# A two-layer hybrid trunk: a block end that transposes x times a scale known one sub-layer ahead

## The chip, the cores and the metric

One core of a Trainium2 chip runs the whole program. The metric is the device time of one execution in microseconds; the figure of a kernel is the median of its runs.

## What is computed

A trunk of two layers over 512 tokens of 1024 features, all in fp32: layer 0 mixes tokens by differential attention, layer 1 by a short gated convolution, and each mixer is followed by a squared-ReLU MLP with 4096 hidden features. Every sub-layer is wrapped in two RMS norms, one ahead of it and one behind it. Shapes left out, it is:

```python
def rmsnorm(x, g):
    return x * lax.rsqrt(jnp.mean(x * x, axis=-1, keepdims=True) + EPS) * g

def short_conv(x, w_in, conv_w, w_out):
    b_gate, c_gate, v = jnp.split(x @ w_in, 3, axis=-1)
    u = c_gate * v                      
    y = conv_w[0] * shift(u, 2) + conv_w[1] * shift(u, 1) + conv_w[2] * u
    return (b_gate * y) @ w_out

def reference(x, ...):
    for i in range(2):
        h = rmsnorm(x, norm_mixer_pre[i])
        m = diff_attention(h, ...) if i == 0 else short_conv(h, ...)
        x = x + rmsnorm(m, norm_mixer_post[i])
        h = rmsnorm(x, norm_mlp_pre[i])
        x = x + rmsnorm(jnp.square(jax.nn.relu(h @ w_up[i])) @ w_down[i], norm_mlp_post[i])
    return x
```

Two facts of it matter here. A norm's factor is one number for each token. And the sub-layers are homogeneous in their input: the MLP and the conv's product `b_gate * c_gate * v` scale with a power of a token's factor (the MLP with the square), and the norm behind the sub-layer divides such a factor out again, but for EPS.

## The kernel before

Every fp32 product is made of three matmuls of rounded parts, hi x hi, lo x hi and hi x lo (`mm3`, lines 66 to 70). ScalarE casts the hi half, VectorE subtracts it from the source for the lo half (`split`, line 199; lines 201 and 202). The stages follow each other in one program: the projections for v and for q and k of eight heads, attention in 32 units, `wo` (the output projection of attention), the MLP of layer 0 (m0), `ci` (the conv's input projection, 24 tiles), `wc` (its output projection) and the MLP of layer 1 (m1). The MLPs' down projection works in seven groups of products into pairs of PSUM banks x, y and z (`down`), which VectorE adds into `acc` (`into`, line 735), and a tail (`tail`) of four token blocks.

`wo`, m0, `wc` and m1 end in `block_end` (line 602), once for each of four blocks of 128 tokens, which applies the norm behind the sub-layer, adds to the residual `x_sb`, applies the norm ahead of the next sub-layer, and has TensorE turn the result into hT, the next stage's operand. Before the change its chain is: two products with `g_post` (line 618), two squares on ScalarE (line 610), two adds on VectorE (lines 612 and 74), a pow on POOL (line 75), x in two halves (line 623); then the same again for x, two squares, two adds and a pow, and hn in two halves (line 632). `turn` holds eight transposes (line 640), two casts on ScalarE for hT_hi (line 643) and two subtractions on VectorE for hT_lo (line 644). It is put into the program some 14 to 22 matmul triples later, by `after`; a scheduler then orders each engine's instructions, and each engine works through its own list in that order.

The first norm (of x itself) is different: v, q and k are projected from x times g, and the token's factor r0 is multiplied in later. For q and k that is in the rope tables, which lie with tokens along the free axis. So r0 has to stand as a row in all partitions, which is a product of a matrix of ones with a diagonal:

```python
    for b in range(NB):
        POOL.tensor_scalar(dg[:, b * P:(b + 1) * P], ident, r0[:, b:b + 1], None, op0=ALU.mult)
    ...
        for b in range(NB):
            PE.matmul(r_ps[:, b * P:(b + 1) * P], lhsT=ones, rhs=dg[:, b * P:(b + 1) * P], start=True, stop=True)
        for j in range(2):
            DVE.tensor_tensor(ropes[:, j], r_ps, ropes[:, j], op=ALU.mult)
```

All loads and stores are issued by SP's queue, in the order of the program.

Of the kernel before, what the change touches and what calls it, by code (L numbers as in the profile page):

```python
# [17 lines left out]
P = 128  # L18
# [24 lines left out]
def trunk(ctx: ExitStack, tc: tile.TileContext, x, xT, w_qk, w_v, w_o, w_in, w_out,  # L43
# [7 lines left out]
    st = ctx.enter_context(tc.tile_pool(name="st", bufs=4))  # L51
    ps = ctx.enter_context(tc.tile_pool(name="ps", bufs=1, space=bass.MemoryType.PSUM))
# [112 lines left out]
    def issue():  # L165
        while n_issued[0] < len(loads):
# [21 lines left out]
            for p in range(2 if first else 1):  # L188
# [5 lines left out]
                if n == "v" and i == p == 0:  # L194
                    nc.sync.dma_start(col, cols)
# [91 lines left out]

    issue()
# [160 lines left out]
    def wo_end(b, o):  # L449
        block_end(f"wo{b}", b, o, norm_rows[0], norm_rows[1], (16, 16, 20, 22)[b])  # L450
# [141 lines left out]
    allowed.append("rawd")  # L592
    issue()
# [8 lines left out]
    def block_end(name, b, parts, g_post, g_next, wait, last=False, cuts=(slice(0, 512), slice(512, 1024))):  # L602


        def mean_square(srcs, tag):

            ss = [small(f"{tag}_{name}_{n}") for n in range(len(srcs))]
            for n, src in enumerate(srcs):
                junk = late.tile([P, 8, 256], F32, tag="F", name=f"jk{tag}_{name}_{n}", bufs=1)
                ACT.activation(junk.rearrange("p a b -> p (a b)")[:, :src.shape[-1]], src, AF.Square, scale=D ** -0.5, accum_out=ss[n])  # L610
                if n < len(srcs) - 1:
                    DVE.tensor_scalar(ss[n], ss[n], EPS if n == 0 else ss[n - 1], None, op0=ALU.add)  # L612
# [284 lines left out]
```

## Time and profile before

| | |
|---|---|
| median of 3 runs | 1118.2 us (1117.86 to 1119.34) |
| the profiled execution | 1119.26 us, its span 1117.4 us |
| TensorE busy | 1096.5 us, 98% |
| VectorE busy | 795.1 us, 71% |
| ScalarE busy | 530.4 us, 47% |
| POOL busy | 101.8 us, 9% |
| TensorE's clock | 0.997 of full speed in the mean |

In rows of the profile PE is TensorE's matmuls, PEld its weight loads, DVE VectorE, ACT ScalarE, POOL GpSimd and SP the queue of the loads. Times count from the start of the span. PEclk is the clock that TensorE was granted, 1.00 being 2.4 GHz and 0.50 1.2 GHz. A row of the timeline gives the start, the time from the first instruction's start to the last one's end, and in brackets how long the engine stood idle before it and what ended that.

### The profile page before, as it was taken

What the parts mean: (1) busy time and instruction counts of PE and PEld (TensorE: products, weight loads), DVE (VectorE), ACT (ScalarE), POOL (GpSimd) and SP (SyncE); (2) the same over time, 40 slices, a digit from 0 to 9 for tenths busy, and PEclk for the clock granted to TensorE, in tenths of its full rate; (3) what the DMA queues carried; (4) which work ended last, traced back from release to release, by engine and by line L of the source; (5) the groups of instructions that cost most, each with busy time, mean ns of one, the idle gap of its engine ahead of it and who ended that gap; (6) DMA issues with size and microseconds to landing.
All of it is one profiled execution on the core that took longest, in us unless ns stands there. A gap on an engine that the chain in (4) does not pass through costs nothing.

```text
span 1117.4 us, 14523 instructions
## 1 busy us (share of the span) xinstructions
PE 1096.5 (98%) x5468; PEld 920.5 (82%) x5468; DVE 795.1 (71%) x1144; ACT 530.4 (47%) x909; POOL 101.8 (9%) x147
## 2 busy tenths in 40 slices
PE   9999999999999999999998999999999999999997
PEld 7878777779888888888888988888988888888886
DVE  6598887455979778878687544446587797797766
ACT  6445555444754554554544422325375445445532
POOL 1144444211000000000001000000000000000000
PEclk9999999999999999999999999999999999999999
DMA  8654444145124314314043332214142242143202
GB/s 307 226 160 124 125 109 128 37 144 197 55 96 151 122 40 140 132 57 151 17 135 114 119 104 98 94 38 143 66 151 75 76 151 95 57 151 111 78 20 76
DMA packets 39447, 124.83 MB, mean 112 GB/s; under 512 B 5072, under 2 KB 5712, under 8 KB 39376
## 3 DMA queue, kind: packets, MB, share of 16 engines
q1 hardware_dynamic: 39376, 123.90, 33.7%
q8 instruction: 43, 0.70, 0.3%
q14 instruction: 28, 0.23, 0.1%
HBM read 111.30 MB, written 2.10 MB: 101 GB/s over the span
## 4 chain that ended last, share of the span: by engine, by line
PE 72%; DVE 3%; issue 2%; POOL 1%; ACT 1%; DMA 0%; POOLq 0%; DVEq 0%; ACTq 0%
PE bank L70 24%; PE bank L69 24%; PE bank L68 24%; DVE x_sb L623 1%; PE bank L640 1%; DVE mg_m L618 0%; DVE acc L779 0%; DVE hn_m L632 0%; DVE lo_up L202 0%; DMA raw_ci<-in_w_in 0%; DVE hT_lo L644 0%; POOL rb_wo L75 0%; POOL rb_m L75 0%; DVE hn_wo L632 0%; POOL ra_m L75 0%
## 5 line engine op out<-in xcount | busy, mean ns | idle before, releaser
L68 PE MATMUL bank<-hT_hi,hi_up 128*128 128x512 f32 (+1 forms) x608 | 216.7, 356 | 0.0
L70 PE MATMUL bank<-hT_hi,lo_up 128*128 128x512 f32 (+1 forms) x608 | 216.5, 356 | 0.0
L69 PE MATMUL bank<-hT_lo,hi_up 128*128 128x512 f32 (+1 forms) x608 | 216.4, 356 | 0.0
L69 PEld LDWEIGHTS bank<-hT_lo,hi_up 128*128 128x128 f32 x608 | 115.0, 189 | 16.3
L68 PEld LDWEIGHTS bank<-hT_hi,hi_up 128*128 128x128 f32 x608 | 115.0, 189 | 16.2
L70 PEld LDWEIGHTS bank<-hT_hi,lo_up 128*128 128x128 f32 x608 | 115.0, 189 | 16.2
L735 DVE TENSOR_TENSOR acc<-acc,bank 128x512 f32<-128x512 f32 x180 | 116.8, 683 | 4.4 <-PE bank L70 4.4
L201 ACT CAST hi_up<-raw_up 128x1024 fp32r<-128x1024 f32 x64 | 67.2, 1054 | 87.2 <-PE bank L70 76.3
L202 DVE TENSOR_TENSOR lo_up<-raw_up,hi_up 128x1024 fp32r<-128x1024 f32 x64 | 76.8, 1220 | 8.7 <-ACT hi_up L201 8.7
L202 DVE TENSOR_TENSOR lo_G<-rawd,hi_G 128x1024 fp32r<-128x1024 f32 x28 | 34.2, 1222 | 44.2 <-ACT hi_G L201 44.2
L69 PE MATMUL bank<-hT_lo,hi_ci 128*128 128x512 f32 (+1 forms) x176 | 62.6, 356 | 1.8 <-DVE b_m L612 1.8
L68 PE MATMUL bank<-hT_hi,hi_ci 128*128 128x512 f32 (+1 forms) x176 | 62.7, 356 | 0.9 <-ACT hT_hi L643 0.8
L70 PE MATMUL bank<-hT_hi,lo_ci 128*128 128x512 f32 (+1 forms) x176 | 62.4, 355 | 0.0
L685 ACT ACTIVATE F<-bank 128x512 f32<-128x512 f32 x64 | 37.6, 593 | 45.0 <-PE bank L70 35.9
L201 ACT CAST hi_G<-rawd 128x1024 fp32r<-128x1024 f32 x28 | 29.5, 1054 | 46.2 <-PE bank L69 31.1
L202 DVE TENSOR_TENSOR lo_E<-rawd,hi_E 128x1024 fp32r<-128x1024 f32 x28 | 34.2, 1222 | 23.4 <-ACT hi_E L201 23.4
L202 DVE TENSOR_TENSOR lo_A<-rawd,hi_A 128x1024 fp32r<-128x1024 f32 x28 | 33.5, 1220 | 19.5 <-ACT hi_A L201 19.5
L201 ACT CAST hi_E<-rawd 128x1024 fp32r<-128x1024 f32 x28 | 29.3, 1048 | 34.9 <-PE bank L69 33.4
L68 PE MATMUL bank<-hi_A,ua_hi 128*128 128x512 f32 x112 | 44.1, 394 | 0.0
L201 ACT CAST hi_A<-rawd 128x1024 fp32r<-128x1024 f32 x28 | 29.5, 1053 | 30.3 <-PE bank L69 17.7
L69 PE MATMUL bank<-lo_A,ua_hi 128*128 128x512 f32 x112 | 43.7, 390 | 0.0
L68 PE MATMUL bank<-hi_E,ub_hi 128*128 128x512 f32 x112 | 43.6, 390 | 0.0
(308 smaller groups left out, 2629.2 us busy)
## 6 DMA issues: line engine op xcount, KB each, us to landing
raw_up<-in_w_up SPq DMA_DIRECT2D x64, 512.0 KB, 4.0
rawd<-in_w_down SPq DMA_DIRECT2D x56, 512.0 KB, 4.4
raw_ci<-in_w_in SPq DMA_DIRECT2D x24, 512.0 KB, 3.5
raw_q<-in_w_qk SPq DMA_DIRECT2D x8, 512.0 KB, 4.5
raw_k<-in_w_qk SPq DMA_DIRECT2D x8, 512.0 KB, 4.3
q<-sw_q SPq DMA_DIRECT2D x32, 128.0 KB, 2.3
raw_wo<-in_w_o SPq DMA_DIRECT2D x8, 512.0 KB, 3.7
raw_dn<-in_w_down SPq DMA_DIRECT2D x8, 512.0 KB, 3.5
```

Of the source, the lines that this page charges most:

```text
L68: PE.matmul(o, lhsT=a[0], rhs=b[0], start=start, stop=False, skip_group_check=more)
L69: PE.matmul(o, lhsT=a[0], rhs=b[1], start=False, stop=False, skip_group_check=more)
L70: PE.matmul(o, lhsT=a[1], rhs=b[0], start=False, stop=stop, skip_group_check=more)
L201: (DVE.tensor_copy if on_dve else ACT.copy)(hi, src)
L202: DVE.tensor_tensor(lo, src, hi.bitcast(F32), op=ALU.subtract)
L623: DVE.scalar_tensor_tensor(xn, m, r, xn, op0=ALU.mult, op1=ALU.add)
L640: PE.transpose(tp[:, j * P:(j + 1) * P], hns[n][:, j * P:(j + 1) * P], ident)
L685: ACT.activation(dst, o, AF.Relu)
L735: DVE.tensor_tensor(a, a, o[t], op=op)
```

## The change

**Block ends.** hn is now x times `s` times `g_next`, where `s` is (ms + 1)^-0.5 with the mean square ms that x had one sub-layer earlier, so it is there before x is. x's own mean square is still taken, by one square of 1024 columns, but off this chain. `settle` forms from it, once a sub-layer's four blocks are done, the factor q = (ms + EPS) s^2 by which hn's square is off, and folds it into the EPS of the next norm behind a sub-layer (power 2 for the MLPs, power 1 for the conv), and for the conv also into a row 1/q, which multiplies the c gate as it leaves PSUM (VectorE, in place of ScalarE's copy). The sums of squares and EPS are added on POOL, ahead of the pow, no longer on VectorE. x and hn are done in one instruction of 1024 columns each (in m1, whose x goes out, in the cuts as before); m0's ends take one square and one product of 1024.

**Rows through memory.** The r0 row and the 1/q row are made by `along_rows`: POOL's DMA queue writes the 128x4 numbers into DRAM in the order of the tokens and reads them back into all partitions. The four `dg` products on TensorE are gone, and VectorE multiplies the rope tables from SBUF.

**Down projection.** The y pair stays in PSUM through all seven groups and into the tail, which goes on adding to it, so two of the adds into `acc` go in each group. The tail's banks are fixed by hand.

**Small ones.** `col` is loaded first, from ScalarE's queue; `rawd` loads are let in a little later.

```diff
-    def rsqrt(r, ms, eps):
-        DVE.tensor_scalar(r, ms, eps, None, op0=ALU.add)
-        POOL.tensor_tensor(r, r, mhalf[:, :ms.shape[-1]], op=ALU.pow)
-        return r
...
-                if n == "v" and i == p == 0:
-                    nc.sync.dma_start(col, cols)
...
+    nc.scalar.dma_start(col, cols)
     issue()
...
+    def along_rows(c, r, name):
+        d = dram.tile([1, T], F32, name=f"row_{name}")
+        POOL.dma_start(d.rearrange("o (b p) -> p (o b)", p=P), c)
+        POOL.dma_start(r, d.partition_broadcast(P))
+        return r
...
+    def scales(ms, name):
+        s = tokens(f"s_{name}")
+        POOL.tensor_scalar(s, ms, 1.0, None, op0=ALU.add)
+        POOL.tensor_tensor(s, s, mhalf, op=ALU.pow)
+        return s
+
+    def settle(name, nxt, power):
+        ms, s, q, e = about["ms", name], about["s", name], tokens(f"q_{name}"), tokens(f"e_{name}")
+        POOL.tensor_scalar(q, ms, EPS, None, op0=ALU.add)
+        for _ in range(2):
+            POOL.tensor_tensor(q, q, s, op=ALU.mult)
+        POOL.tensor_scalar(e, q, EPS, None, op0=ALU.mult)
+        if power == 1:
+            POOL.tensor_tensor(q, q, mone, op=ALU.pow)
+            about["row"] = along_rows(q, acc[:, 2, 0:T], "q")
+        else:
+            POOL.tensor_tensor(e, e, q, op=ALU.mult)
+        about["eps", nxt] = e
+        if nxt != "m1":
+            about["s", nxt] = scales(ms, nxt)
...
+        if kt == 6:
+            r0 = small("r0", 4)
+            POOL.tensor_scalar(r0, ss0, EPS, None, op0=ALU.add)
+            POOL.tensor_tensor(r0, r0, mhalf, op=ALU.pow)
+            about["s", "wo"] = scales(ss0, "wo")
+            r_row = along_rows(r0, t512(ap, "r_row", "c", 2), "r0")
...
-            DVE.tensor_tensor(ropes[:, j], r_ps, ropes[:, j], op=ALU.mult)
+            DVE.tensor_tensor(ropes[:, j], r_row, ropes[:, j], op=ALU.mult)
...
+        m = late.tile([P, D], F32, tag="mg", name=f"mg_{name}_{b}", bufs=1)
+        for p, c in zip(parts, cuts):
+            DVE.tensor_tensor(m[:, c], p, g_post[:, c], op=ALU.mult)
+        for n, src in enumerate(parts):
+            ss = small(f"ss_{name}_{b}_{n}")
+            mean_square(ss, src, n)
+            if n:
+                POOL.tensor_tensor(r, ss, r, op=ALU.add)
+            elif ("eps", name) in about:
+                POOL.tensor_tensor(r, ss, about["eps", name][:, b:b + 1], op=ALU.add)
+            else:
+                POOL.tensor_scalar(r, ss, EPS, None, op0=ALU.add)
+        POOL.tensor_tensor(r, r, mhalf[:, 0:1], op=ALU.pow)
+        xb = x_sb[:, b, :]
+        for c in cuts if last else (slice(0, D),):
+            DVE.scalar_tensor_tensor(xb[:, c], m[:, c], r, xb[:, c], op0=ALU.mult, op1=ALU.add)
...
-        r2 = mean_square([x_sb[:, b, c] for c in cuts], "b")
...
+        hn = late.tile([P, D], F32, tag="hn", name=f"hn_{name}_{b}", bufs=2)
+        DVE.scalar_tensor_tensor(hn, xb, about["s", name][:, b:b + 1], g_next, op0=ALU.mult, op1=ALU.mult)
+        if b == 0:
+            about["ms", name] = tokens(f"ms_{name}")
+        mean_square(about["ms", name][:, b:b + 1], xb, "x")
+        if b == NB - 1:
+            settle(name, nxt, power)
...
-            product(g, y, True, "A12", "A", 1)
-            into((1, 1), y, ALU.add)
+            product(g, y, new, "A12", "A", 1)
...
+                spare = [(z[0], z[1]), (x[0], x[1]), (y[0], z[0]), (y[1], z[1], x[0])][b]
+                spare = list(spare)
                 for run in runs:
-                    os = [bank() for c in run]
+                    os = [spare.pop(0) for c in run]
...
-            ACT.copy(held["c"], o)
+            DVE.tensor_tensor(held["c"], o, about["row"], op=ALU.mult)
```

What this does to the order of instructions is seen at three places. The first is VectorE in the projections, between the last step for lambda (`neg_lam`) and the rope tables; `lo_` and `both_` are lo halves of weights, `acc<-bank` and `acc<-pair` the evictions of v. Before:

```order
L368 TENSOR_SCALAR neg_lam<-neg_lam 128x1
L202 TENSOR_TENSOR lo_q_595<-raw_q_463,hi_q_594 128x512 x2
L202 TENSOR_TENSOR lo_k_684<-raw_k_508,hi_k_683 128x512 x2
L202 TENSOR_TENSOR both_q_780<-raw_q_555,both_q_780 128x512 x2
L348 TENSOR_SCALAR acc<-bank_71,r_424 128x512
L348 TENSOR_SCALAR acc<-pair_77,r_424 128x512
L348 TENSOR_SCALAR acc<-pair_78,r_424 128x512
L348 TENSOR_SCALAR acc<-bank_73,r_424 128x512
L202 TENSOR_TENSOR both_k_888<-raw_k_600,both_k_888 128x512 x2
L355 TENSOR_TENSOR ropes<-bank_73,ropes 128x512 x2
```

With the change:

```order
L400 TENSOR_SCALAR neg_lam<-neg_lam 128x1
L387 TENSOR_TENSOR ropes<-r_row,ropes 128x512 x2
L195 TENSOR_TENSOR lo_q_597<-raw_q_469,hi_q_596 128x512 x2
L195 TENSOR_TENSOR lo_k_686<-raw_k_510,hi_k_685 128x512 x2
L195 TENSOR_TENSOR both_q_782<-raw_q_557,both_q_782 128x512 x2
L383 TENSOR_SCALAR acc<-bank_73,r_395 128x512
```

The two rope products have moved from behind the evictions and a further pair of lo halves to ahead of three pairs and the evictions.

The second is TensorE in the last run of `wo`'s block 2, where block 0's transposes (`ident,hn_wo`) are put in. Before:

```order
L70 MATMUL pair_77<-both_wo_2079,oT_lo 128x512
L68 MATMUL pair_77<-both_wo_2079,oT_hi 128x512
L69 MATMUL pair_77<-both_wo_2079,oT_hi 128x512
L70 MATMUL pair_77<-both_wo_2079,oT_lo 128x512
L68 MATMUL pair_77<-both_wo_2105,oT_hi 128x512
L640 MATMUL bank_72<-ident,hn_wo_0_2391 128x128 x4
L69 MATMUL pair_77<-both_wo_2105,oT_hi 128x512
L640 MATMUL bank_73<-ident,hn_wo_1_2393 128x128 x4
L70 MATMUL pair_77<-both_wo_2105,oT_lo 128x512
L68 MATMUL pair_77<-both_wo_2105,oT_hi 128x512
L69 MATMUL pair_77<-both_wo_2105,oT_hi 128x512
L70 MATMUL pair_77<-both_wo_2105,oT_lo 128x512
```

With the change:

```order
L69 MATMUL pair_79<-both_wo_2081,oT_hi 128x512
L70 MATMUL pair_79<-both_wo_2081,oT_hi 128x512
L673 MATMUL bank_74<-ident,hn_wo_2381 128x128 x4
L673 MATMUL bank_75<-ident,hn_wo_2381 128x128 x4
L71 MATMUL pair_79<-both_wo_2081,oT_lo 128x512
L69 MATMUL pair_79<-both_wo_2081,oT_hi 128x512
L70 MATMUL pair_79<-both_wo_2081,oT_hi 128x512
L71 MATMUL pair_79<-both_wo_2081,oT_lo 128x512
L69 MATMUL pair_79<-both_wo_2107,oT_hi 128x512
L70 MATMUL pair_79<-both_wo_2107,oT_hi 128x512
```

The eight transposes stand together, after two matmuls of the last run of twelve instead of after seven. Those of block 1 stand 21 matmuls behind block 0's, those of block 2 33 matmuls behind block 1's.

The third is VectorE in m0's ends, from block 2's product with `g_post` to block 1's hT_lo (two instructions), the first of which TensorE needs for the conv's first tile. Before:

```order
L618 TENSOR_TENSOR mg_m_2_1_5153<-acc,g_post_2619 128x512
L612 TENSOR_SCALAR a_m_2_0_5155<-a_m_2_0_5155 128x1
L202 TENSOR_TENSOR lo_ci_5252<-raw_ci_4994,hi_ci_5251 128x1024
L74 TENSOR_SCALAR ra_m_2_5162<-a_m_2_1_5156,a_m_2_0_5155 128x1
L779 TENSOR_TENSOR acc<-bank_2617,acc 128x512
L623 SCALAR_TENSOR_TENSOR x_sb<-mg_m_2_0_5151,ra_m_2_5162,x_sb 128x512
L623 SCALAR_TENSOR_TENSOR x_sb<-mg_m_2_1_5153,ra_m_2_5162,x_sb 128x512
L644 TENSOR_TENSOR hT_lo<-bank_72,hT_hi 128x4x128
L612 TENSOR_SCALAR b_m_2_0_5167<-b_m_2_0_5167 128x1
L644 TENSOR_TENSOR hT_lo<-bank_73,hT_hi 128x4x128
```

With the change:

```order
L643 TENSOR_TENSOR mg_m_2_5070<-acc,g_post_2584 128x1024
L195 TENSOR_TENSOR lo_ci_5149<-raw_ci_4945,hi_ci_5148 128x1024
L656 SCALAR_TENSOR_TENSOR x_sb<-mg_m_2_5070,r_m_2_5069,x_sb 128x1024
L195 TENSOR_TENSOR lo_ci_5179<-raw_ci_4956,hi_ci_5178 128x1024
L662 SCALAR_TENSOR_TENSOR hn_m_2_5078<-x_sb,s_m_2573,g_pre_2586 128x1024
L677 TENSOR_TENSOR hT_lo<-bank_74,hT_hi 128x4x128
L677 TENSOR_TENSOR hT_lo<-bank_75,hT_hi 128x4x128
```

Block 1's hT_lo stood behind one `lo_ci`, an add from a bank and x in two halves; now it stands behind two `lo_ci`, x and hn, and the add comes later.

## Rows read from the trace of the kernel before

**Rows 1.** The page's first part: busy us, share of the span, instructions.

```profile
PE 1096.5 (98%) x5468; PEld 920.5 (82%) x5468; DVE 795.1 (71%) x1144; ACT 530.4 (47%) x909; POOL 101.8 (9%) x147
```

**Rows 2.** Stretches: length, busy us of each engine (instructions), PEclk, DMA share, GB/s.

```profile
220.00:240.00 20.00, 18.50 (x92) 15.15 (x91) 7.26 (x17) 5.09 (x16) 2.60 (x6) 1.00 0.44 158
230.00:237.00 7.00, 7.00 (x32) 5.81 (x31) 3.22 (x7) 2.50 (x7) 0.55 (x1) 1.00 0.99 379
...
620.00:1100.00 480.00, 480.00 (x2319) 405.20 (x2318) 323.57 (x421) 211.08 (x290) 4.94 (x9) 1.00 0.28 96
```

**Rows 3.** TensorE's waits in the whole run: who waited for whom: us, times, longest.

```profile
PE bank L640 <- DVE hn_wo L632: 2.8, 3, 1.5
PE bank L69 <- DVE b_m L612: 1.8, 1, 1.8
```

**Rows 4.** Stretches again, where m0's end meets the conv.

```profile
591.00:595.00 4.00, 1.31 (x7) 0.80 (x6) 3.87 (x8) 2.60 (x7) 0.55 (x1) 1.00 0.37 130
595.00:600.00 5.00, 5.00 (x30) 5.00 (x31) 4.87 (x9) 2.56 (x7) 0.55 (x1) 0.66 0.01 3
607.00:609.00 2.00, 1.57 (x15) 1.37 (x14) 1.42 (x2) 0.15 (x1) 0.31 (x1) 1.00 0.89 274
```

**Rows 5.** Timeline of block 0's `wo` end, VectorE and TensorE: start us, us, instruction [idle before].

```profile
235.00 1.42 DVE L623 SCALAR_TENSOR_TENSOR x_sb<-mg_wo,ra_wo,x_sb 128x512 f32<-128x512 f32 x2 [0.66 <-POOL ra_wo L75]
...
238.23 1.42 DVE L632 SCALAR_TENSOR_TENSOR hn_wo<-x_sb,rb_wo,g_pre 128x512 f32<-128x512 f32 x2
...
239.13 0.63 PE L640 MATMUL bank<-ident,hn_wo 128*128 128x128 f32 x4 [1.50 <-DVE hn_wo L632]
```

**Rows 6.** Timeline of TensorE at the `dg` products.

```profile
51.93 1.05 PE L353 MATMUL bank<-dg,ones 128*128 128x128 f32 x8
52.74 0.47 PE L68 MATMUL bank<-hT_hi,hi_q 128*128 128x512 f32 x1
```

**Rows 7.** Timeline of ScalarE: the last 1024-wide square.

```profile
32.37 1.06 ACT L332 ACTIVATE xb<-xb 128x1024 f32<-128x1024 f32 x1 [0.90 <-DMA xb<-in_x]
```

**Rows 8.** Groups by line and shape, POOL: busy us, mean ns, idle before.

```profile
L532 POOL TENSOR_SCALAR f<-eps 128x4 f32<-128x4 f32 x7 | 1.6, 228 | 0.6
```

**Rows 9.** Timeline of POOL: two of the pows.

```profile
234.42 0.55 POOL L75 TENSOR_TENSOR ra_wo<-ra_wo,mhalf 128x1 f32<-128x1 f32 x1 [8.85 <-DVE ra_wo L74]
...
247.02 1.46 POOL L75 TENSOR_TENSOR rb_wo<-rb_wo,mhalf 128x1 f32<-128x1 f32 x1 [4.04 <-DVE rb_wo L74]
```

**Rows 10.** DMA issues: count, KB each, us to landing.

```profile
x_sb<-in_x SPq DMA_DIRECT2D x4, 512.0 KB, 7.4
...
col<-in_cols SPq DMA_DIRECT2D x1, 16.5 KB, 2.7
```

**Rows 11.** Timeline of VectorE in the projections.

```profile
44.63 1.30 DVE L202 TENSOR_TENSOR both_q<-raw_q,both_q 128x512 fp32r<-128x512 f32 x2 [2.56 <-ACT both_q L201]
45.84 0.74 DVE L348 TENSOR_SCALAR acc<-bank,r 128x512 f32<-128x512 f32 x1
...
55.77 0.74 DVE L380 STREAM_SHUFFLE sw_q<-bank 128x512 f32<-128x512 f32 x1
```

**Rows 12.** Groups by line and shape, VectorE.

```profile
L735 DVE TENSOR_TENSOR acc<-acc,bank 128x512 f32<-128x512 f32 x180 | 116.8, 683 | 4.4 <-PE bank L70 4.4
L202 DVE TENSOR_TENSOR lo_up<-raw_up,hi_up 128x1024 fp32r<-128x1024 f32 x64 | 76.8, 1220 | 8.7 <-ACT hi_up L201 8.7
```

**Rows 13.** Timeline of VectorE in m0's ends.

```profile
583.94 1.41 DVE L623 SCALAR_TENSOR_TENSOR x_sb<-mg_m,ra_m,x_sb 128x512 f32<-128x512 f32 x2 [0.73 <-POOL ra_m L75]
...
594.18 0.68 DVE L644 TENSOR_TENSOR hT_lo<-bank,hT_hi 128x512 fp32r<-128x512 f32 x1
```

**Rows 14.** Timeline in the conv: ScalarE's first gate copy, TensorE's first 512-wide tile.

```profile
619.48 0.58 ACT L809 COPY conv<-bank 128x512 f32<-128x512 f32 x1
...
632.84 0.40 PE L68 MATMUL bank<-hT_hi,hi_ci 128*128 128x512 f32 x1
```

**Rows 15.** Timeline of VectorE: the last x.

```profile
1114.17 0.49 DVE L623 SCALAR_TENSOR_TENSOR x_sb<-mg_m,ra_m,x_sb 128x256 f32<-128x256 f32 x1
```

More of the change, by code (lines that the diff above doesn't have):

```diff
@@ L599, in row, with block_end, mean_square @@
         return r
[L602 to L612, printed above, removed]
-            return rsqrt(small(f"r{tag}_{name}"), ss[-1], ss[-2])
-        mg = []
-        for n, (p, c) in enumerate(zip(parts, cuts)):
-            m = t512(late, f"mg_{name}_{n}", "mg", 2)[:, :c.stop - c.start]
-            DVE.tensor_tensor(m, p, g_post[:, c], op=ALU.mult)
-            mg.append(m)
-        r = mean_square(parts, "a")
-        for m, c in zip(mg, cuts):
-            xn = x_sb[:, b, c]
-            DVE.scalar_tensor_tensor(xn, m, r, xn, op0=ALU.mult, op1=ALU.add)
+    def block_end(name, nxt, power, b, parts, g_post, g_next, wait, last=False, cuts=(slice(0, 512), slice(512, 1024))):
+        def mean_square(ss, src, n=0):
+            junk = late.tile([P, 8, 256], F32, tag="F", name=f"jk_{name}_{b}_{n}", bufs=1)
+            ACT.activation(junk.rearrange("p a b -> p (a b)")[:, :src.shape[-1]], src, AF.Square, scale=D ** -0.5, accum_out=ss)
+        r = small(f"r_{name}_{b}")
+        m = late.tile([P, D], F32, tag="mg", name=f"mg_{name}_{b}", bufs=1)
[14 more added lines that the diff above has]
+            DVE.scalar_tensor_tensor(xb[:, c], m[:, c], r, xb[:, c], op0=ALU.mult, op1=ALU.add)
@@ L716, in finish @@
                 us[n, p] = [x[:, j, :] for x in t]
+        x, y, z = ([banks[2 * i], banks[2 * i + 1]] for i in range(3))
         def product(g, o, first, form, kind, half):
@@ L725, in product @@
                     step(lambda: mm3(o[t], part(us[form, p], ALL, slice(t * P, (t + 1) * P)), part(w, ALL, s),
-                                     first and p == groups[g][0], p == groups[g][-1], not first))
+                                     first and p == groups[g][0], p == groups[g][-1] and o is not y,
+                                     not first and o is not y))
         def into(c, o, op, fresh=False):
@@ L737, in down @@
         def down(g):
-            x, y, z = ([banks[2 * i], banks[2 * i + 1]] for i in range(3))
             new, pq = g == 0, groups[g]
@@ L779, in tail @@
                         DVE.tensor_tensor(a, o, a, op=ALU.add)
-                cuts = [c for run in runs for c in run]
-                block_end(f"m{l}_{b}", b, [acc[:, b, c] for c in cuts], g_post, g_next, 14, last=l == 1, cuts=cuts)
+                cuts = [c for run in runs for c in run] if l else [slice(0, D)]
+                block_end(f"m{l}", "wc", 1, b, [acc[:, b, c] for c in cuts], g_post, g_next, 14, last=l == 1, cuts=cuts)
         for n, what in mlp_steps:
```

33 lines of the change are left out of this document (13 added, 20 removed).

## The prediction

> **What bounds the kernel now.** Read the busy times first: TensorE works in 1096.5 of 1117.4 us [rows 1]. The program is therefore as long as TensorE's own list of matmuls plus about 21 us of gaps, and an edit pays only if it takes matmuls out, closes a gap, or shortens the end behind the last matmul. The table of stretches then says where gaps can be: from 620 to 1100 us TensorE is busy in all 480.00 us, though 2319 matmuls run there beside 421 VectorE instructions [rows 2]. Whatever VectorE saves in the MLPs, in the later conv tiles and in the ends of `wc` is worth nothing. The list of waits names what is left to this change: the transposes of the `wo` ends wait 2.8 us for `hn_wo`, and around the ends of the first MLP (m0) TensorE waits 1.8 us for what stands behind b_m, block 1's hT_lo [rows 3]. The stretches there show the price: 1.31 us busy in the 4 us from 591, so 2.7 us of nothing, then 5 us fully busy at a granted clock of 0.66, so 5.00 x 0.34 = 1.7 us more, then 0.43 us missing in 607 to 609 [rows 4]. The clock was at its upper level (2.4 GHz) before that gap and near the lower one (1.2 GHz) for some us behind it; the 1.5 us gap in `wo` [rows 5] left it at 1.00 in that whole stretch [rows 2]. Last comes the tail behind the last matmul, where VectorE's x is the last link [rows 15].
>
> **The change, part by part**, in the time of the profiled execution (1119.26 us, of which the span is 1117.4; it lies 1.06 us above the median of 1118.2).
>
> *Rope row.* The four fp32 products with `dg` go: the next matmul starts 52.74 - 51.93 = 0.81 us after them [rows 6], with TensorE busy on both sides. That is -0.8, for all that follows starts earlier; if a later gap swallows half, -0.4. New is a row by way of memory, which VectorE awaits ahead of three pairs of `lo` (1.30 each) and of the eviction of the V bank that k's first projection needs, not behind them. The last square ends by 33.5 [rows 7]; an add (0.23 [rows 8]) and a pow on POOL (0.55, or up to 1.46 [rows 9]), with those of `s` between, give 35. No DMA issued by POOL is in this trace. The nearest rows are 2.7 us to landing for the smallest transfer (16.5 KB) and 7.4 for rows of x at a busy time [rows 10]: two in sequence, 5.4 to 14.8, land the row at 40.5 to 50. I take the lower end, since one is smaller than `col` and the other half as large as a weight tile. Behind the wait stand 1.29 + 3 x 1.30 + 0.74 = 5.9 us [rows 11]; q's projection hands over to k's at about 55.6, when VectorE shuffles it [rows 11], so a row by 49 costs nothing: 8 us of cover.
>
> *Ends of `wo`.* Block 0's factor comes as before (pow ends at 234.97 [rows 9]), since the squares, two adds (now on POOL, 0.2 each [rows 8]) and one pow follow the same transfer. What goes is x's square, its two adds and its pow: 238.23 - 236.42 = 1.8 us between x and hn [rows 5]. A 1024-wide multiply takes 1.22 where two of 512 take 0.68 each [rows 12]; for the three-operand form (0.75) that makes an estimated 0.75 + 0.54 = 1.3. So x ends at 236.3, hn at 237.6. But the order puts the transposes five matmuls earlier as well, 5 x 0.227 us (some 31 matmuls in the 7.00 us from 230, the first and the last cut by the edge [rows 2]), from 237.63 (239.13 less its wait [rows 5]) to 236.5: they wait 1.1 us, not 1.5. In blocks 1 and 2 they again move up by more than hn does: 8 transposes and 21 matmuls behind block 0's is 243.3, and hn comes at 244.3 (ACT squares b1 only behind x's wide square and two hT_hi); 33 matmuls on is 252.8, with hn at 253.8. Three waits of about 1 us replace 2.8 in all, and the interleaved halves lose their switch between transposes and matmuls: 0 +- 0.5. **The shorter chain is spent by the earlier position.**
>
> *m0 into the conv.* hn0 comes earlier and both groups of transposes lose the wait for their second half. That only brings TensorE earlier to the same gap. What ends the gap is block 1's hT_lo (594.18 to 594.86 now [rows 13]), and in the new order it stands behind mg2, `lo_ci`, x2, another `lo_ci` and hn2, where it stood behind `lo_ci`, an add and x2. By durations: x1 ends at 583.7 (583.94 + 1.41 = 585.35 before [rows 13]; hn0, ahead of it, no longer waits for a pow and ends 3 us sooner); its square on ACT 1.06 [rows 7] and some 0.2 for its sum; two hT_hi, 586.1; two hT_lo and an add, 587.4; mg2 588.6; `lo_ci` 589.8, under which POOL's add and pow are held up (0.55 alone, 1.46 beside such a `lo` [rows 9]), so r2 at 590.5; x2 591.7, `lo_ci` 592.9, hn2 594.1, hT_lo 594.7. So the gap and the low clock behind it stay, -0.1; the 0.43 us in 607 to 609 goes, since hn3 needs no pow behind two `lo_ci`. Together -0.5; the ends are +1.5 (two held-up POOL steps) and -3 (below).
>
> *Gate.* The product with the row replaces a copy on ACT (0.58 at 619.48 [rows 14]) by 0.69 on VectorE, eight times. q needs seven small POOL steps behind x3's square at 603.5, so about 607, and two transfers: 612 to 622. The gate wants it at 619; what TensorE wants is only the bank, at 632.84 [rows 14]. Ten us of cover, cost nothing; if that is gone, each further us of the row is a us of TensorE's.
>
> *MLP.* 28 of 180 adds of 683 ns [rows 12] go, 19 us of VectorE: nothing, because of the 480.00 above.
>
> *Tail.* All three mg stand before r in the new order, so the last x (1114.17 to 1114.66 now [rows 15]) loses the mg of 256 columns ahead of it, 0.68 - 0.27 = 0.41 by rows 12; and with the sums on POOL VectorE reaches the last adds and with them r some 0.35 us sooner. -0.75; 0 if the banks and not VectorE set them, -1 at most. *Start:* `col` first in ACT's queue, -0.1 +- 0.3, since hi_v is late too.
>
> **Sum**: -0.8 + 0 - 0.5 - 0.75 - 0.1 = -2.15 us, 1117.1 for an execution like the profiled one, **1116.0** beside the median. A measurement of this kernel tells about 0.2%, 2.2 us, from no change: 1116.0 is that border, and so the two sides of it share this case.
>
> **Rivals.** *No gain:* the shift of 0.8 is swallowed by the gaps of attention, and the tail is set by the banks. For it: TensorE in m0 waits on VectorE's order, not on itself. 1117.0 to 1118.5.
>
> *The gap shrinks and the clock stays up.* If block 1's hT_lo ends at 593.5 (POOL not held up, wide forms at 1.2), the gap is near the 1.5 us that left the clock at 1.00 in `wo`: -1.2 and -1.7, so about 1113. Against it: five instructions of 1.2 us each stand between 587 and hT_lo.
>
> *Slower: the rope row comes late.* The place is VectorE's wait behind `neg_lam`; from a landing at 49 on, each us is TensorE's, and weights' raw buffers behind it come free later too. At 51 the whole gain is gone, at 53.5 the kernel is slower by 0.2%; a row at 55 gives 1116.0 + 6 = 1122. For it: POOL has no DMA in this trace, so its price is unknown, the write is 512 elements of 4 B, and POOL is held up beside VectorE (0.55 to 1.46 [rows 9]) in just the stretch where VectorE runs its pairs of `lo`. Against: VectorE stands idle for 2.56 us there [rows 11].
> The Trainium skill, "SBUF — State Buffer", section "SBUF: two separate sides", speaks against this change: while VectorE runs an operation in a two-port mode, GpSimd can't write the descriptors of its own DMAs, and a DMA from the ACT or SP queue would not wait. By that rule both transfers of the row start only in gaps between VectorE's instructions, at about 38 and 43, and land near 46, which takes most of the cover: this rival at its mild end. The same page ("Who interferes with whom") gives a two-input product only the shared read side, and infers that it doesn't stop descriptors; by that the row lands as I take it. The held-up pow agrees with the read side, and no row here shows a DMA of POOL's.
>
> **How the numbers follow.** Forecast 0.52 (1114.8 to 1117.4, a little more than half of it beyond the border), no gain 0.17, clock 0.13, slower 0.18 (the late row 0.12, for an unknown price beside 8 us of cover; an m0 gap longer by POOL's held-up steps 0.06). Faster: 0.30 + 0.13 = 0.43; same: 0.22 + 0.17 = 0.39; slower 0.18. The range drops the deeper half of the clock case and most of the late row: 1112.0 to 1120.0.
>
> **What would show it.** After: no matmul between q's and k's first projection; `ropes` multiplied before 49; L640's waits in `wo` still about 3 us; a gap of some 3 us near 591 to 595 and the clock under 1.00 behind it; none near 607; 620 to 1100 still full; the last x about 0.75 us closer to the last matmul. Wrong would be: a wait of VectorE on POOL's DMA that TensorE repeats (the slower case), 1.00 all through 595 to 600 (the clock case), or gaps in the MLPs.

## The result, and the profile after

The changed kernel takes 1137.1 us in the median of 5 runs (1135.33 to 1138.42), the kernel before beside it 1119.3 us: a ratio of 1.0156, with a 95% interval from 1.0145 to 1.0168. It is 17.7 us slower. The prediction was 1116.0 us, its range ended at 1120.0, and slower had 0.18. It was wrong in sign and in size.

The profiled execution after took 1135.33 us (span 1133.2). Its busy line, as in [rows 1]:

```profile
PE 1108.9 (98%) x5460; PEld 920.2 (81%) x5460; DVE 775.0 (68%) x1038; ACT 521.6 (46%) x869; POOL 111.4 (10%) x187
```

Three groups of TensorE's matmuls by line and shape, with the columns of [rows 12]:

```profile
L71 PE MATMUL bank<-hT_hi,lo_up 128*128 128x512 f32 x416 | 165.6, 398 | 0.0
L70 PE MATMUL bank<-hT_lo,hi_up 128*128 128x512 f32 x416 | 164.3, 395 | 0.0
L69 PE MATMUL bank<-hT_hi,hi_up 128*128 128x512 f32 x416 | 163.4, 393 | 0.0
```

TensorE's waits, as in [rows 3]:

```profile
PE pair L503 <- DMA k<-t_k: 3.2, 1, 3.2
PE bank L70 <- DVE hT_lo L677: 3.0, 1, 3.0
PE bank L673 <- DVE hn_wo L662: 2.8, 3, 1.5
...
PE bank L69 <- ACT hT_hi L676: 1.5, 1, 1.5
```

The DMA issues of the rows, as in [rows 10]:

```profile
r_row<-row_r POOLq DMA_DIRECT2D x1, 256.0 KB, 4.2
...
row_r<-r POOLq DMA_DIRECT2D x1, 2.0 KB, 10.2
```

TensorE has 8 matmuls fewer than in [rows 1] and is busy 12.4 us longer, though the granted clock in the mean is 0.997 as before and the stretch from 620 to 1100 us is full in both. The span grew by 15.8 us, so most of the time did not go into waits: the matmuls themselves take longer. One of the same three groups in the kernel before (the other two have the same mean):

```profile
L68 PE MATMUL bank<-hT_hi,hi_up 128*128 128x512 f32 x416 | 162.0, 389 | 0.0
```

And one stretch of 400 us without a gap, of the kernel before and then of the changed one:

```profile
700.00:1100.00 400.00, 400.00 (x1915) 336.73 (x1914) 282.94 (x375) 183.42 (x255) 4.94 (x9) 1.00 0.27 93
```

```profile
700.00:1100.00 400.00, 400.00 (x1890) 332.04 (x1889) 268.99 (x328) 181.75 (x241) 5.64 (x17) 1.00 0.28 94
```

389 ns became 393 to 398 ns (these durations overlap in the pipeline; the starts of the 1248 `up` products of 512 columns lie 0.2267 us apart in the mean before and 0.2335 after). In the same 400 us 25 matmuls fewer get done, at a clock of 1.00. From start to start, products of E, G, D and `wc` moved by 0.5 ns at most and those of A by 1.6; slower by 4 to 7 ns are `up`, `ci`, v, q and k, all of which read hT beside a weight tile.

Smaller losses stand at two places that the prediction named. In the projections, on POOL and on VectorE:

```profile
36.24 1.00 POOL L306 DMA_DIRECT2D row_r<-r  x1
...
46.73 0.59 POOL L307 DMA_DIRECT2D r_row<-row_r  x1 [9.50 <-DMA row_r<-r]
```

```profile
50.92 1.29 DVE L387 TENSOR_TENSOR ropes<-r_row,ropes 128x512 f32<-128x512 f32 x2 [13.08 <-DMA r_row<-row_r]
...
59.59 0.75 DVE L412 STREAM_SHUFFLE sw_q<-bank 128x512 f32<-128x512 f32 x1
```

The row is there at 50.9, and q is shuffled at 59.6 instead of 55.8 [rows 11]. At m0's end, ScalarE, then VectorE (blocks 0 and 1), then POOL, and the stretches with TensorE's busy time first:

```profile
597.92 1.98 ACT L194 CAST hi_ci<-raw_ci 128x1024 fp32r<-128x1024 f32 x2
599.81 0.57 ACT L676 CAST hT_hi<-bank 128x512 fp32r<-128x512 f32 x1
```

```profile
587.07 1.28 DVE L662 SCALAR_TENSOR_TENSOR hn_m<-x_sb,s_m,g_pre 128x1024 f32<-128x1024 f32 x1
588.27 1.28 DVE L818 TENSOR_TENSOR acc<-bank,acc 128x512 f32<-128x512 f32 x2
...
591.75 1.28 DVE L656 SCALAR_TENSOR_TENSOR x_sb<-mg_m,r_m,x_sb 128x1024 f32<-128x1024 f32 x1 [0.94 <-POOL r_m L653]
...
603.39 1.28 DVE L677 TENSOR_TENSOR hT_lo<-bank,hT_hi 128x512 fp32r<-128x512 f32 x2
```

```profile
598.10 1.10 POOL L650 TENSOR_TENSOR r_m<-ss_m,e_wo 128x1 f32<-128x1 f32 x1 [6.38 <-ACT jk_m L637]
```

```profile
598.00:603.00 5.00, 1.69 (x9) 0.99 (x7) 4.29 (x5) 4.15 (x8) 1.65 (x2) 1.00 0.34 110
603.00:608.00 5.00, 3.87 (x20) 3.87 (x21) 5.00 (x7) 1.95 (x3) 0.79 (x1) 0.66 0.33 105
```

The gap that was 2.7 us of nothing in four [rows 4] is now 3.3 in five and goes on behind 603, 4.4 us in two waits. The granted clock is 0.66 in the stretch behind it, as it was before.

### The profile page after: what moved, and what is told of

Its sections match the earlier page's. It is cut to its first block, busy times and chain, and to the rows that moved or that the text cites. A ratio compares the mean times of both kernels' runs of the same rounds, so it can differ in the third digit from the quotient of the medians.

```text
span 1133.2 us, 14411 instructions
## 1 busy us (share of the span) xinstructions
PE 1108.9 (98%) x5460; PEld 920.2 (81%) x5460; DVE 775.0 (68%) x1038; ACT 521.6 (46%) x869; POOL 111.4 (10%) x187
## 4 chain that ended last, share of the span: by engine, by line
PE 78%; DVE 7%; DMA 6%; issue 3%; ACT 3%; POOL 2%; SPq 1%; POOLq 0%; DVEq 0%; ACTq 0%
PE bank L71 25%; PE bank L69 25%; PE bank L70 25%; DMA xb<-in_x 1%; DVE a L536 1%; DMA raw_v<-in_w_v 1%; PE bank L552 1%; DMA q_lo<-t_q 1%; DMA raw_ci<-in_w_in 1%; PE bank L673 1%; DVE x_sb L656 1%; DMA raw_wo<-in_w_o 1%; ACT p L518 0%; DMA x_sb<-in_x 0%; POOL t_k L416 0%
## 5 line engine op out<-in xcount | busy, mean ns | idle before, releaser
L71 PE MATMUL bank<-hT_hi,lo_up 128*128 128x512 f32 (+1 forms) x608 | 219.8, 361 | 0.0
L774 DVE TENSOR_TENSOR acc<-acc,bank 128x512 f32<-128x512 f32 x152 | 100.3, 682 | 11.9 <-PE bank L71 10.8
L194 ACT CAST hi_G<-rawd 128x1024 fp32r<-128x1024 f32 x28 | 29.5, 1052 | 50.4 <-PE bank L70 34.7
L70 PE MATMUL bank<-lo_E,ub_hi 128*128 128x512 f32 x112 | 43.6, 389 | 0.0
```

The source lines that it names most:

```text
L70: PE.matmul(o, lhsT=a[0], rhs=b[1], start=False, stop=False, skip_group_check=more)
L71: PE.matmul(o, lhsT=a[1], rhs=b[0], start=False, stop=stop, skip_group_check=more)
L194: (DVE.tensor_copy if on_dve else ACT.copy)(hi, src)
L774: DVE.tensor_tensor(a, a, o[t], op=op)
```

## The experiments

Ratios are against the kernel before on the same chip. The questions: why do matmuls slow down, what does the row cost and why, and what makes the gap at m0's end. Diffs are cut to the edit.

**1. Why the matmuls take longer.** The weights' pool lies in each partition behind the tiles of constants, of which hT is the first. With every tile rounded up to 32 bytes they add up, in the kernel before, to 3 x 16384 (two of hT, `acc`) + 160 (`col`) + 512 (`ident`) + 3 x 32 = 49920 bytes from hT to the weights, a multiple of 256. The change puts 13 more small tiles there, 32 bytes each, which makes it 50336, 160 more than a multiple of 256. The theory was that this distance sets the pitch; the rival was the changed instruction stream.

```diff
+    pad = const.tile([P, 1], F32, name="pad")
+    POOL.memset(pad, 0.0)
```

These two lines, in the kernel before, behind the small constants:

> The kernel before with one more tile of 32 bytes a partition behind the small constants, so that the pools of weights, u and the attention's tiles lie 32 bytes further on, while hT stays where it is; one memset of POOL is the only new instruction. Theory (operands): a 512-column matmul that reads hT as one operand and a weight as the other takes 6.7 ns longer when the two differ by 32 bytes modulo 64; 2256 of them make about 15 us, so 1133 to 1134, TensorE's busy time about 1111, the up products at 0.2333 us a matmul instead of 0.2267. Rival (the changed instruction stream slows TensorE: its new DMAs, the y banks that stay open, VectorE's wider forms): nothing of that is here, so 1118 to 1119 and 0.2267.

Measured: 1131.5 us, ratio 1.0113 (1.0098 to 1.0128); `up` at 0.2333 us from start to start. The busy line:

```profile
PE 1108.7 (98%) x5468; PEld 918.8 (81%) x5468; DVE 795.2 (70%) x1144; ACT 530.7 (47%) x909; POOL 102.4 (9%) x148
```

One unread tile of 32 bytes costs the kernel before 12 us, some 2 less than the theory had. The same lines ahead of hT:

> The same tile of 32 bytes, but ahead of hT: hT, weights, u and the attention's tiles all lie 32 bytes further on. Theory in its relative form (only a difference between the two operands costs): 1118 to 1119.5, busy 1096.5. In its absolute form (an operand that doesn't begin at a multiple of 64 costs, whatever the other does): at least as slow as the version with the tile last, 1133 or more, since now all products are affected. Rival (instruction stream): 1118 to 1119.

Measured: 1119.7 us, ratio 1.0006 (0.9997 to 1.0015), busy 1098.1, 0.2267. What counts is the distance between the two operands, not the place of either. Then the changed kernel, with the same tile behind its constants, and with one of 24 numbers (96 bytes):

> The changed kernel with a 32-byte tile behind its small constants, which brings weights, u and the attention's tiles back to the same place modulo 64 as hT. Theory (operands): 15 us come back, 1121 to 1122.5 instead of 1137.1, up products at 0.2267; what is left above the kernel before is the late rope row (some 2 us) and the longer gap of the first MLP's end (some 2 us), less the dg products. Rival (instruction stream): 1137, busy 1109.

Measured: 1125.2 us, 1.0058 (1.0043 to 1.0073), busy 1100.6, but `up` at 0.2290. The theory held in direction and missed by 3 us: 0 modulo 64 is not enough.

> The changed kernel with a tile of 96 bytes a partition behind its small constants: the distance from hT to the weights is again 0 modulo 128, as in the kernel before (with 32 bytes it was 64 modulo 128, and a 512-column product took 0.2290 us there, against 0.2267 before and 0.2333 in the changed kernel). Theory (the price goes by the distance modulo 128 or more): 0.2267 again, 5 us less than with the 32-byte tile, of which 256-column products give back up to 1.7 (0.1178 there, 0.1199 before): 1120 to 1122. Rival (0.2290 is what the changed instruction stream costs once the 32-byte offset is gone): 1125 and 0.2290.

Measured: 1124.2 us, 1.0039 (1.0026 to 1.0052); `up` 0.2267, busy 1096.8. The pitch is back, and the time is 2 us above what was expected. What is left against the kernel before, 0.39% or 4.4 us, lies at the two places named. TensorE's busy time from 52 to 100 us, before and here:

```profile
52.00:100.00 48.00, 46.68 (x246) 38.01 (x245) 39.88 (x68) 21.55 (x63) 21.17 (x22) 1.00 0.54 146
```

```profile
52.00:100.00 48.00, 42.46 (x205) 34.51 (x204) 41.13 (x70) 19.23 (x56) 17.94 (x19) 0.93 0.57 163
```

From 580 to 620 us it is 36.87 before and 35.78 here. So the row costs more than the expectation's sum had for it, about 2 us; experiments 2, 3 and 5 look at that.

> No part of the trunk: x is copied to the output, and TensorE runs 20 series of 72 fp32r products of three kinds as in the MLPs (moving 128 x 512 or 128 x 256 from one tile, stationary 128 x 128 from another), each series with another distance between the two operands' first bytes: 0 to 224 in steps of 32, for 512 and for 256 columns; then both operands shifted by 32 and by 96, the moving one alone by 32, and 0 again. Theory (distance modulo 128): 0.2267 us a product of 512 at 0 and 128, 0.2333 at 32 and 160, 0.2290 at 64 and 192; both shifted alike 0.2267; moving alone by 32 not 0.2267. Rival (the absolute place of one operand counts): both shifted by 32 as slow as one. If all series agree at 0.2267, the distance is not the cause.

Measured, on TensorE's timeline (B has distance 0, C to I have 32 to 224 from the moving operand on to the stationary one, J and K are 256 columns at 0 and 32, R and S have both operands shifted, T the moving one alone, U has 0 again):

```profile
34.55 16.26 PE L72 MATMUL oB<-mov,sta 128*128 128x512 f32 x71
50.65 16.95 PE L72 MATMUL oC<-mov,sta 128*128 128x512 f32 x72
67.44 16.96 PE L72 MATMUL oD<-mov,sta 128*128 128x512 f32 x72
84.25 17.02 PE L72 MATMUL oE<-mov,sta 128*128 128x512 f32 x72
101.11 16.89 PE L72 MATMUL oF<-mov,sta 128*128 128x512 f32 x72
117.83 16.96 PE L72 MATMUL oG<-mov,sta 128*128 128x512 f32 x72
134.64 16.65 PE L72 MATMUL oH<-mov,sta 128*128 128x512 f32 x72
151.13 16.96 PE L72 MATMUL oI<-mov,sta 128*128 128x512 f32 x72
167.93 8.79 PE L72 MATMUL oJ<-mov,sta 128*128 128x256 f32 x72
176.56 8.68 PE L72 MATMUL oK<-mov,sta 128*128 128x256 f32 x72
...
236.16 16.55 PE L72 MATMUL oR<-mov,sta 128*128 128x512 f32 x72
252.54 16.53 PE L72 MATMUL oS<-mov,sta 128*128 128x512 f32 x72
268.91 16.96 PE L72 MATMUL oT<-mov,sta 128*128 128x512 f32 x72
285.71 16.50 PE L72 MATMUL oU<-mov,sta 128*128 128x512 f32 x72
```

From start to start a product of 512 takes (50.65 - 34.55) / 71 = 0.2268 us at distance 0, (67.44 - 50.65) / 72 = 0.2332 at 32, 0.2335 at 64, 0.2342 at 96, 0.2322 at 128, 0.2335 at 160, 0.2290 at 192 and 0.2333 at 224; both operands shifted alike 0.2275, the moving one alone 0.2333. The expected repeat at 128 is not there: of the distances tried, only 0 modulo 256 is fast. That agrees with `up` in every kernel here (0: 0.2267; 32: 0.2333; 160: 0.2335; 192: 0.2290). It agrees with v too, which has hT as its stationary operand, so that its distance counts the other way: in the version with the 32-byte tile `up` has 192 and v 64, and v's products stayed at 0.2333. Why the distance counts isn't shown.

**2. What the row costs.** Four dg products in place of the row, in the version with the 32-byte tile:

```diff
-            r_row = along_rows(r0, t512(ap, "r_row", "c", 2), "r0")
+            dg = t512(ap, "dg", "c", 2)
+            for b in range(NB):
+                POOL.tensor_scalar(dg[:, b * P:(b + 1) * P], ident, r0[:, b:b + 1], None, op0=ALU.mult)
```

> The version before this one in the list (changed kernel, operands brought into line) with the r0 row made as it was in the kernel before, by four products with dg on TensorE, the row's two DMAs gone. Theory (the row comes late and TensorE waits for it): the wait for k's rotated tile goes back from 3.2 to about 1.0 us, the products cost 0.8, so 1.4 to 2.2 us less than the version with the row: about 1119.5 to 1120.5. Rival (VectorE's wait is hidden, TensorE never waits for it): 0.8 us more than the version with the row, about 1122.5.

Measured: 1124.0 us, 1.0038 (1.0026 to 1.0050): 1.3 us less, with intervals that overlap, while the wait for k's tile went from 3.7 to 0.9 us in the profiles. This pair alone is inconclusive (the six runs with the row spread from 1123.7 to 1129.4); a later one (experiment 3) gives 4.5. Then the queue, with `nc.scalar` in place of `POOL` in `along_rows`:

> As the version with the 96-byte tile, but the four DMAs of the two rows are issued by ScalarE's queue instead of POOL's. Theory (POOL's path is slow: 10.2 us for 2 KB written): the write lands in about 3 us, VectorE's wait for the r0 row shrinks from 13 to about 6 us, TensorE's wait for k's rotated tile from 3.2 to 1.0: 2 to 2.8 us less. Rival (512 elements of 4 bytes take that long on any queue): the write again takes 9 to 10 us, time the same within 0.5 us.

Measured: 1127.6 us, 1.0068 (1.0053 to 1.0083), slower than with POOL's queue. The write, then VectorE, ScalarE and a stretch:

```profile
row_r<-r ACTq DMA_DIRECT2D x1, 2.0 KB, 9.6
```

```profile
46.69 0.69 DVE L387 TENSOR_TENSOR ropes<-r_row,ropes 128x512 f32<-128x512 f32 x1 [1.59 <-DMA r_row<-row_r]
```

```profile
618.67 1.07 ACT L678 CAST hT_hi<-bank 128x512 fp32r<-128x512 f32 x2 [14.00 <-DMA row_q<-q_m]
```

```profile
580.00:620.00 40.00, 32.54 (x215) 29.99 (x213) 23.21 (x27) 14.64 (x24) 8.29 (x14) 0.91 0.24 83
```

The write takes as long on this queue: the rival's cause holds, though not its time. The row lands at 46.7 instead of 51.1, since its write is issued at 33.2 instead of 37.8, and TensorE's wait for k's tile is 0.8. Most of that is not the queue's doing: the sum of the last square reached POOL 3.4 us sooner in this execution. But the gate's row stops ScalarE for 14.00 us ahead of a cast that TensorE needs, and that is where this version loses.

By the Trainium skill, "SBUF — State Buffer", section "SBUF: two separate sides", a DMA of POOL's queue is held up while VectorE runs an operation in a two-port mode, and one of ScalarE's queue is not. No run here shows such a difference: the write of r0 took 8.8 to 10.4 us from issue to landing on POOL's queue and 9.6 to 10.1 on ScalarE's. VectorE stood idle through most of the writes on POOL's queue, so the rule was not put to the test. What makes the write slow:

> No part of the trunk: x is copied to the output, and ahead of it 2 KB are written from SBUF to memory and read back into all partitions, one pair after the other, twice over, on SP's and on POOL's queue, in three layouts of the write: as the row does it (512 pieces of 4 bytes), 128 pieces of 16 bytes, and one piece of 2 KB from one partition. Theory (the number of pieces): 8 to 10 us for the first, about 3 to 4 for the second, 2 to 3 for the third, alike on both queues. Rival (a write into memory costs that whatever its layout): 8 to 10 us for all three. Rival (POOL's queue): SP's writes at 2 to 3 us.

```profile
bpsp<-src SPq DMA_DIRECT2D x2, 2.0 KB, 9.1
pbsp<-src SPq DMA_DIRECT2D x2, 2.0 KB, 1.9
...
bppool<-src POOLq DMA_DIRECT2D x2, 2.0 KB, 8.4
pbpool<-src POOLq DMA_DIRECT2D x2, 2.0 KB, 1.7
onepool<-src POOLq DMA_DIRECT2D x2, 2.0 KB, 1.6
```

These are its DMA issues (`bp` is the row's layout, `pb` the one of 128 pieces, `one` the single piece). 512 pieces of 4 bytes cost 8.4 to 9.1 us, the same 2 KB in 128 pieces 1.7 to 1.9, in one piece 1.6: the layout is the price. The Trainium skill, "DMA: Bandwidth & Descriptors", section "Anatomy of one DMA — SWDGE (gpsimd) path", gives a DMA of POOL's queue about 2.0 us and a part by bytes, an estimate of 2.0 us here. On that queue the last two layouts come a little under it (1.7 and 1.6), the first takes four times as much.

**3. The order at m0's end.** In `turn`, for m0, the casts and subtractions of hT get priority over the next block's x and hn, and the turn comes 12 triples behind the block's end, not 14:

```diff
-                ACT.copy(hT[0][:, ks, ts], tpv)
-                DVE.tensor_tensor(hT[1][:, ks, ts], tpv, hT[0][:, ks, ts].bitcast(F32), op=ALU.subtract)
+                with tc.high_priority() if name == "m0" else nullcontext():
+                    ACT.copy(hT[0][:, ks, ts], tpv)
+                    DVE.tensor_tensor(hT[1][:, ks, ts], tpv, hT[0][:, ks, ts].bitcast(F32), op=ALU.subtract)
```

> As the version with the 96-byte tile, with the r0 row made by the four products with dg again, and in the first MLP's ends the two casts and two subtractions that make hT put ahead of the next block's x and hn (by priority in the order, and by a turn 12 triples after the block's end instead of 14). Theory (the gap at the conv's start is the order of VectorE's and ScalarE's lists): the waits of 3.0 and 1.5 us shrink to under 1 us together, the clock stays at 1.00 from 592 to 600: 3 to 5 us less by this, 1.3 by dg, so 1115 to 1117, faster than the kernel before. Rival (the chain from the block's matmuls to hT is as long as the gap whatever the order): waits of 3 us or more, 1119 to 1120.

Measured: 1114.2 us, 0.9949 (0.9937 to 0.9961), faster than the kernel before, and 10 us below the version with the 96-byte tile where 4.3 to 6.3 were expected. From 580 to 620 us:

```profile
580.00:620.00 40.00, 39.07 (x290) 36.52 (x289) 23.33 (x27) 16.89 (x26) 10.61 (x16) 1.00 0.27 87
```

> The version with the order of the first MLP's ends mended and operands at distance 0 (1114.2 us), but with the r0 row through memory on POOL's queue as in the change, in place of the four dg products. Theory (the row lands at 51, past the deadline of 49, and TensorE repeats it twice, at V's banks and at k's tile, the clock going down behind it): 1.3 to 5 us more, 1115.5 to 1119. Rival (TensorE never waits for the row): 0.8 us less, 1113.4.

Measured: 1118.7 us, 0.9995 (0.9986 to 1.0003). So the row costs 4.5 us against dg (0.46% by the ratios, 5 us), not the 1.3 that the earlier pair gave, and the order is worth 1.0039 - 0.9995, 0.44% or 5 us. Both together are worth 0.90%, 10 us; by the earlier pair the order's part would be larger and the row's smaller, so the sum is surer than the division.

> The kernel before with one edit: the casts and subtractions that make hT in the first MLP's ends have priority in the order; the long chain (x's own square, two adds and a pow ahead of hn) stays, and the turn stays 14 triples behind the block's end. Theory (the order of VectorE's list is all there is to the gap): its waits of 1.8 and 0.8 us and the low clock behind them go, 3 to 4.5 us less, 1115 to 1117. Rival (the short chain of the change is needed, for hT can't come early while hn waits for a pow): 1.5 us less or nothing, 1118 to 1120.

Measured: 1117.5 us, 0.9985 (0.9976 to 0.9993): 1.7 us, between the two. The clock stays at 1.00, but TensorE now waits for `hn_m`, which still waits for a pow:

```profile
PE bank L640 <- DVE hn_m L632: 1.8, 3, 1.0
```

That speaks for the change's shorter chain being worth something here, once the order lets it through. How much isn't shown: beside the chain, this run and the two above differ in the place of the turn (14 triples, not 12).

**4. The position in wo, the down projection.** The list of what is due is no longer emptied ahead of `wo`'s last row, and the waits of the turns are (9, 11, 19, 22) in place of (16, 16, 20, 22):

```diff
-                while k not in tiles or (due and name == "wo" and k == KT - 1):
+                while k not in tiles or (due and not opened and name == "wo" and k == KT - 1):
```

> The version with the order mended, operands at distance 0 and dg products (1114.2 us), with the transposes of wo's ends 7, 10 and 18 or more matmuls further back in TensorE's list (the output projection no longer empties the list of what is due ahead of its last row). Theory (the prediction's: the shorter chain of wo's ends is spent by an earlier position of the transposes): their waits of 2.5 us in all go, 2 to 2.5 us less, 1111.7 to 1112.2. Rival (what follows is paced by the same chain): the wait comes back at the MLP's first matmul or in the next block, no change within 0.5 us.

Measured: 1111.5 us, 0.9929 (0.9916 to 0.9941); no wait for `hn_wo` is left, and from 235 to 270 us TensorE is busy 34.97 of 35 us.

> The version with the order mended, operands at distance 0 and dg products (1114.2 us), with the down projection as before the change: the y pair is added into acc in every group, 28 adds of 0.68 us more on VectorE. Theory (the prediction's: TensorE never waits in the MLPs, so the adds are worth nothing): the same within 0.5 us. Rival (open y banks take VectorE's load off TensorE's path): up to 19 us more if nothing covered them, over 1 us more if some of it counts.

Measured: 1114.8 us, 0.9958 (0.9946 to 0.9970), 0.6 us from 1114.2 and within its interval. The adds are worth nothing that these runs can tell.

**5. Where the row is awaited.** The row's write alone on ScalarE's queue, the read-back on POOL's:

> The version with the later transposes of wo (1111.5 us) with the r0 row through memory again in place of the dg products, its write issued by ScalarE's queue (which then waits for nothing more) and its read-back by POOL's, so that neither queue holds up an engine; the gate's row as in the change. Theory (a row that lands by 49 us costs nothing, and the dg products are worth 0.8): lands at about 47.5, TensorE's wait for k's tile 0.8 to 1.0, 0.5 to 0.8 less, 1110.7 to 1111.0. Rival (VectorE's wait ahead of the pairs of lo and of V's evictions costs TensorE also when the row lands at 47.5): 1 to 4 us more.

Measured: 1115.9 us, 0.9965 (0.9952 to 0.9979), 4.5 us more than with dg (0.36% by the ratios, 4 us). The row lands at 49.3, almost the prediction's 49, and q is shuffled at 58.0: a row by 49 does cost. The landing at 47.5 that the theory expected was not reached (with both DMAs on POOL's queue, in experiment 3, it was 49.3 too), so what a row at 47.5 would cost stays open. Last, the two products behind V's last eviction, the row as in the change:

```diff
+        with tc.issue_after(evicted.ins):
             for j in range(2):
                 DVE.tensor_tensor(ropes[:, j], r_row, ropes[:, j], op=ALU.mult)
```

> The version with the later transposes of wo (1111.5 us with dg products), with the r0 row through memory on POOL's queue exactly as in the change, but with the two products with the rope tables put behind V's last eviction in VectorE's list, one pair of lo ahead of the shuffle of q, where they stood ahead of three pairs and the evictions. Theory (the place of the wait is what costs: from the row's use to the shuffle stand 8.7 us of VectorE's work in the change, here about 2.5): the row lands at about 50 to 51, the shuffle of q is on time at about 56, TensorE's wait for k's tile is 0.8 to 1.0, its clock 1.00 from 52 to 100, and the dg products' 0.8 is gained: 1110.5 to 1111. Rival (the row itself is too slow, wherever it is awaited): 1113 to 1116, as with the write on ScalarE's queue.

Measured: 1110.5 us, 0.9929 (0.9915 to 0.9943), the fastest version here, though not told apart from the one with dg by the ratios. VectorE and TensorE there:

```profile
51.39 1.28 DVE L388 TENSOR_TENSOR ropes<-r_row,ropes 128x512 f32<-128x512 f32 x2
...
54.96 0.74 DVE L415 STREAM_SHUFFLE sw_q<-bank 128x512 f32<-128x512 f32 x1
```

```profile
52.00:100.00 48.00, 46.74 (x244) 38.00 (x243) 41.44 (x71) 21.55 (x63) 21.20 (x22) 1.00 0.56 154
```

VectorE no longer stands idle for the row, and the shuffle waits for TensorE's bank, not the other way round. The row lands at 50.4, against 50.9 in the change and 49.3 where it cost 4 to 5 us, and now costs nothing.

## Why the prediction was wrong

**The step that failed by most** is its first: "The program is therefore as long as TensorE's own list of matmuls plus about 21 us of gaps". The list of matmuls was right (8 fewer); that the others would keep their durations was taken for granted, and the term stood at nothing. From start to start the 1680 products of 512 columns of `up` and `ci` take 6.6 to 6.8 ns more, 11.3 us, v's 192 about 7 ns, 1.4 us, q's and k's 288 about 4 ns, 1.2 us. The version with the 96-byte tile gives 13 us back (1.0156 to 1.0039). Neither the forecast nor a rival had a place for it, since the change adds no work to those products.

**Rope row, -0.8.** Its rival came, "Slower: the rope row comes late": the row cost 4.5 us against dg in experiment 3, and 1.3 in the less sure pair of experiment 2. Two numbers of it were wrong. The price: two DMAs "5.4 to 14.8, land the row at 40.5 to 50. I take the lower end", and they took 10.2 and 4.2, the upper one; the reason given (2 KB is smaller than `col`) looked at bytes, where the pieces count. And the cover: "a row by 49 costs nothing" counted 5.9 us of VectorE behind the wait, up to the eviction that k's projection needs. The shuffle of q stands behind three more evictions and a pair for k as well, 59.59 - 50.92 = 8.7 us. With the hand-over at 55.6 the row was due at 47: at 46.7 TensorE's wait for k's tile was as before, at 49.3 the row cost 4.5 us. Beside the wait itself the clock fell, to 0.96 or 0.93 between 52 and 100 us in four of the executions with a late row (not in the change's own, where it stayed at 1.00), so "each us is TensorE's" was too low as well.

**wo, 0 +- 0.5.** Right: three waits of 2.8 us as before, and the run with later transposes shows the reason named, the earlier position, to be the cause.

**m0 into the conv, -0.5.** Wrong in sign. That x2, a `lo_ci` and hn2 stand ahead of hT_lo was seen, and so was POOL's step held up beside a `lo` (1.10 us for an add). That part came to the tenth: from the end of x1 to the end of the first half of hT_lo the prediction has 594.7 - 583.7 = 11.0 us, the trace 604.07 - 593.03 = 11.0. The step that failed is the start, "x1 ends at 583.7". VectorE before:

```profile
578.98 0.68 DVE L779 TENSOR_TENSOR acc<-bank,acc 128x512 f32<-128x512 f32 x1
...
580.82 1.41 DVE L632 SCALAR_TENSOR_TENSOR hn_m<-x_sb,rb_m,g_pre 128x512 f32<-128x512 f32 x2 [0.44 <-POOL acc L802]
```

Block 1's adds into `acc` stood ahead of hn0, in the time in which hn0 waited for its pow; in the change they stand behind it (588.27). So hn0 came 1.7 us sooner, not 3, counted from TensorE's last product ahead of the gap (which starts at 590.71 before and at 598.57 after), but block 1's square and with it r1 came no sooner: x1 ended 5.5 us ahead of that product, as before (5.4), where the prediction had 7.0. What was not followed either is ScalarE's list: the first half of hT_hi stood behind two casts of `hi_ci`. TensorE waited 1.5 us for it and 3.0 us for hT_lo, instead of 0.8 and 1.8. The 0.43 us near 607 did go: TensorE is busy in all of the 10 us from 608. In the changed kernel, order and the turn's place were worth 5 us.

**MLP and gate, 0.** The run with the old down projection bears the first out. The gate's row came at 630.7. Its first step on POOL began at 612.8 where the prediction had about 603.5, so this is 621.4 by the prediction's times, inside its 612 to 622, and TensorE did not wait for it.

**Tail, -0.75.** From the last matmul's start to the end it is 1133.2 - 1125.70 = 7.5 us, and was 1117.4 - 1109.77 = 7.6: 0.1, not 0.75. The last x did end 0.5 us closer to the last matmul (4.4 us behind its start, not 4.9), but from there to the end it took 3.1 us instead of 2.7; why isn't shown. The last three x still follow POOL's last add and pow, and these follow the last bank.

**Start, -0.1.** v's first product starts at 4.94 us, and did at 4.95: nothing.

## What to carry to other kernels

A new tile, even one of 32 bytes, moves every pool behind it, so compare the start-to-start time of unchanged matmuls in two profiles before reading anything else, and keep the distance of a product's two operands where it was. A transfer of a few KB is priced by its pieces before its bytes, and its deadline is found by counting everything that stands behind the wait in the waiting engine's list, up to the last instruction that somebody needs. A chain that gets shorter pays only if the order of all engines on it, the casts too, lets the result through.

## What was not expected of the hardware

A product of 512 columns takes 0.2267 us when its two operands begin a multiple of 256 bytes apart, 0.2290 at 192 more and 0.232 to 0.234 at the other distances tried (steps of 32 bytes). With 256 columns distance 0 is not the fast one: 0.1199 there, 0.1200 at 160, and 0.1174 to 0.1186 at the others; in the change (160) such products of `up` took what they took before. Why isn't settled. A write of 512 pieces of 4 bytes took 8.4 to 10.4 us on three queues, the same bytes in 128 pieces 1.7 to 1.9.
